# Parameters loaded with the first k-tiles, transposes placed behind ten products, other homes for three buffers, and a last output tile in two products of 256 columns

## The chip, the cores and the metric

The kernel runs on one NeuronCore of a Trainium2 chip. The metric is the device time of one execution in microseconds (us), lower is better. The engines are TensorE (PE in the profile; PEld is its weight load, which overlaps the products), VectorE (DVE), ScalarE (ACT), GpSimd (POOL) and SyncE (SP), on whose queue nearly all transfers are issued. Each engine and each queue works in the order in which its instructions stand.

## The reference

One layer of a streaming encoder on `x` of 1024 positions by 1024 features, all float32. One input projection gives four blocks of 512 columns: `u` for a diagonal state-space group (S5), `q` and `k` together, `v`, and a gate for a retention group of four heads. The parts around the change are these:

```python
lam_bar = jnp.exp(lam * dt); b_bar = ((lam_bar - 1.0) / lam)[..., None] * b
bu = jnp.einsum('blgc,gpc->blgp', u, b_bar)          # then an associative scan over positions
...
y = jnp.concatenate([y_s5, y_ret], -1) @ w_out
x = layer_norm(ALPHA * x + y, ln1_g, ln1_b)
ffn = (silu(conv3(x @ w_up_a)) * (x @ w_up_g)) @ w_down
x = layer_norm(ALPHA * x + ffn, ln2_g, ln2_b)
```

## The kernel before, in words

Every large product is made from float32 operands split into a high and a low part (ACT casts the high part, DVE subtracts it), three products of 128 rows by 512 columns for each pair of tiles (`mm3`, L132). The input projection runs block by block, `u` (block 0), `v` (2), `q,k` (1), gate (3), over four pairs of k-tiles (`project`, L195). For each pair `load_w` (L169) fetches two raw weight tiles through three rotating buffers `wraw` and splits them into `wsp<block>_<pair>`; in block 0 it fetches and splits `x` as well.

While `u` is multiplied, `load_constants` (L276, called by `project` after the second pair) puts the loads of the S5 parameters on SP, `par3` (lambda and step, 48 KB) first and `par` (B and C, 1 MB) later. DVE then works out powers of the discretised lambda in small operations of 32 to 256 columns (L324 to L407, scratch in `scr`), and from these the table `W` of two halves (L415 to L425): for each half a multiply into `W<h>`, a multiply into `Wt<h>`, and an add, 2048 columns each. The products of `u` leave PSUM in eight ACT copies into `U0` and `U1` (L293), go to a scratch `uscr` in DRAM in four stores (L294), two for each of `U0` and `U1`, and come back rearranged as `UT0`, `UT1` (L299). A load of `d` into the second quarter of `par` (L491, written far later in the program) has to wait until DVE has read that quarter in the two `Wt` multiplies (L422).

During the first two pairs of block `v` only seven of the eight PSUM banks hold `v`; through the eighth (`small`, L236) pass, between the products, eight `make_BT` (L447: four transposes of `W`, then one ACT copy into `BT0` or `BT1`; quarters 0 to 3 are BT0's) in the first pair and eight `make_V` (L461: products of `BT` with `UT`, ACT copies into `V2`) in the second. `spread_out(..., 5)` asks for one of them every five products, and the first pair has 42 products in all.

Buffers of 8 KB a partition come from an `Arena` (L73), a first-in first-out list of 20 slots: `free` puts a slot at the end, `get` takes the one that has been free longest, and the new tile's first writer waits for the last reader of the old one. Counted through, `BT0` takes the slot of `Wt1`, `BT1` that of `U0`, `wsp2_2` that of `U1`, `scan` that of `Wt0`.

The order of each engine's instructions is set when the program is built, by a planner: among the instructions that are ready on its own clock it takes the one that stands first in the program, with the weight loads and splits of blocks 1 to 3 moved ahead (`high_priority(HP)`). So an instruction written later can stand earlier in a queue when the planner believes it ready.

At the end (L1314 to L1327) four output tiles of 128 rows are completed one after the other, each by 33 products of 512 columns (`down_mm`) added to the high half of `zw[0][:, i]`. Ahead of them in the program stands `layer_norm_far` (L869) for four other tiles. Tiles 0 and 1 then use `layer_norm` (L863: DVE statistics, POOL's power -0.5, one DVE operation, one ACT scaling, one POOL addition), tiles 2 and 3 `layer_norm_last` (L886: the same statistics and power, then three DVE operations and two stores).

Of the kernel before, what the change touches and what calls it, by code (L numbers as in the profile page):

```python
# [12 lines left out]
F32 = mybir.dt.float32  # L13
F32R = mybir.dt.float32r
# [6 lines left out]
P = 128  # L21
# [7 lines left out]
EPS = 1e-5  # L29
# [77 lines left out]
def layer_kernel(ctx, tc, a, out):  # L107
# [87 lines left out]
    def project(blk, ops, banks, between=(), after=None, mid=None):  # L195


        ws = []
        late = len(between) > 0
        for kp in range(4):  # L200
            with tc.high_priority(0 if blk == 0 else HP):
                w, n = load_w(blk, kp)
            todo = deque(between[kp]) if late and kp < 2 else deque()
            ws.append(w)
            for q in range(2):
                k = 2 * kp + q
                if k < 7:
                    for (xi_, wi_) in ((0, 0), (0, 1), (1, 0)):
                        for j in range(7 if late and kp < 2 else 8):
                            l, r = ops(w[:, q], k, j, xi_, wi_)  # L210
                            T.matmul(banks[j], lhsT=l, rhs=r, start=(k == 0 and xi_ == 0 and wi_ == 0), stop=False)  # L211
                            if todo:
                                todo.popleft()()
                else:
                    for j in range(8):
                        proj3(banks[j], ops, w[:, q], k, j, False, True)
            assert not todo
            if mid is not None and kp == 1:
                mid()
            if late and kp < 2:  # L220
                if kp == 0:
                    continue
                if after is not None:
                    after()
                banks[7] = small("late")
                for k in range(4):
                    wk = ws[k // 2][:, k % 2]
                    proj3(banks[7], ops, wk, k, 7, k == 0, False)
                A.free(f"wsp{blk}_0")
            A.free(n)  # L230
            if blk == 3:
                A.free(f"x{2 * kp}", f"x{2 * kp + 1}")
# [11 lines left out]
    def spread_out(groups, n):  # L244

        return [g for gr in groups for g in [gr] + [lambda: None] * (n - 1)]
# [26 lines left out]
    pw = A.get([P, 2048], F32, "pw")  # L273
    par3 = pw[:, 1600:1696]

    def load_constants():  # L276
        SP.dma_start(par3, a["s5p"][:, 2048:S_END])
        SP.dma_start(con, a["con"])
        SP.dma_start(ident, a["ident"])
        SP.dma_start(par, a["s5p"][:, 0:2048])  # L280
        SP.dma_start(gains, a["gains"])
# [133 lines left out]

    A.free("scr")
    W = []
    for h in range(2):
        w_ = A.get([P, 16, 8, 16], F32, f"W{h}")
        t_ = A.get([P, 16, 8, 16], F32, f"Wt{h}")  # L420
        V.tensor_mul(w_, rev_pow(KR, 16 * h), vec_b(par[:, S_B1:S_B1 + 512], 16 * h))
        V.tensor_mul(t_, rev_pow(KIs, 16 * h), vec_b(par[:, S_B2:S_B2 + 512], 16 * h))  # L422
        V.tensor_add(w_, w_, t_)
        A.free(f"Wt{h}")
        W.append(w_)  # L425

    UT = []
    for h in range(2):
        UT.append(load_UT(h, f"UT{h}"))
        A.free(f"U{h}")  # L430

    scan = A.get([P, 4, 2, 256], F32, "scan")
    t1s = [scan[:, h] for h in range(2)]
# [27 lines left out]
    def make_V(i):  # L461
        h, q = i // 4, i % 4
        b_ = small(f"v{h}{q}")
        for e in range(4):
# [4 lines left out]


    banks = [bank(f"v_{b}") for b in range(7)] + [None]
    project(2, ops_b, banks, [spread_out([partial(make_BT, q) for q in range(8)], 5),
                              spread_out([partial(make_V, i) for i in range(8)], 5)])
    A.free("BT0", "BT1", "UT0", "UT1")
    vt = [A.get([P, 4, 512], F32, f"vt{h}") for h in range(2)]
# [120 lines left out]
    def glu_weights():  # L596
        r = A.get([P, 4, 512], F32, "glr")
        SP.dma_start(r, a["glu_w"])
        glh = A.get([P, 4, 512], F32R, "glh")
        gll = A.get([P, 4, 512], F32R, "gll")  # L600
        for k in range(4):
            S.copy(glh[:, k], r[:, k])
            V.tensor_sub(gll[:, k], r[:, k], f32(glh[:, k]))
        A.free("glr")
        return glh, gll

    glw = []
    banks = [bank(f"g_{b}") for b in range(8)]
    project(3, ops_b, banks, mid=lambda: glw.extend(glu_weights()))
    glh, gll = glw  # L610


# [250 lines left out]
    def layer_norm(z, lnv, pool, i):  # L863
        mv, rs = norm_stats(z, pool, i)
        V.scalar_tensor_tensor(z, z, mv[:, 0:1], lnv[:, 0], ALU.subtract, ALU.mult)
        S.activation(z, z, AF.Copy, scale=rs)  # L866
        G.tensor_add(z, z, lnv[:, 1])  # L867
# [446 lines left out]
    for m in range(NP):  # L1314
        down_prep_last(m)
    layer_norm_far([zw[1][:, i] for i in range(4)], lnv, cp, lambda i: SP.dma_start(outb(4 + i), zw[1][:, i]))
    for i in range(4):
        b_ = bank(f"dn3{i}")
        for m in range(NP):
            down_mm(b_, *dops[3, m], i, m == 0, m == NP - 1)  # L1320
        z, cs = zw[0][:, i], slice(512, 1024)
        V.tensor_add(z[:, cs], z[:, cs], b_)
        if i < 2:
            layer_norm(z, lnv, cp, f"b{i}")
            SP.dma_start(outb(i), z)
        else:
            layer_norm_last(z, lnv, cp, f"b{i}", lambda q, cs: (SP, S)[q].dma_start(outb(i)[:, cs], z[:, cs]))  # L1327


_ORDER = ["con", "ident", "xT", "xn", "w_in", "s5p", "d", "glu_w", "glu_b", "gains", "w_out",  # L1330
# [50 lines left out]
```

## Time and profile before

| | |
|---|---|
| median of 3 runs | 1027.43 us (1026.75 to 1028.75) |
| the profiled execution's own time | 1028.04 us |
| its span | 1026.3 us |
| PE busy in the span | 1004.3 us (98%) |
| DVE, ACT, POOL busy | 796.4, 447.7, 49.6 us |
| mean granted clock of TensorE | 0.993 of full speed |

All times in the rows are counted from the start of the span. A row of a timeline gives its start, the time from the first start to the last end of what was merged in it, the engine, the line, the operation, the tiles written and read, and, in brackets, how long the engine had been idle and which engine's instruction ended that.

### The profile page before, as it was taken

The page shows a single profiled execution, that of the slowest core. Times are in us where ns is not written, and L with a number is a line of the kernel's source. Part 1 is how long each engine was busy: PE and PEld are TensorE (multiplying, and loading weights), DVE is VectorE, ACT ScalarE, POOL GpSimd, SP SyncE. Part 2 cuts the span into 40 slices and gives each one's busy share as a digit, 9 for nine tenths or more (in the row PEclk, how much of TensorE's full clock was granted, in tenths as well). Part 3 has the DMA queues.
Part 4 walks back from the last instruction along what each step waited for, and adds up shares of the span by engine and source line. Part 5 has one row for each costly group of instructions (what it writes and reads, how often), then busy time and mean ns, then how long its engine had stood idle before and what let it go on. Part 6 is the DMA issues. An engine that isn't in the chain of part 4 may idle for free.

```text
span 1026.3 us, 12781 instructions
## 1 busy us (share of the span) xinstructions
PE 1004.3 (98%) x4748; PEld 828.7 (81%) x4748; DVE 796.4 (78%) x1376; ACT 447.7 (44%) x778; POOL 49.6 (5%) x60
## 2 busy tenths in 40 slices
PE   9989999999999999999999999999999999999996
PEld 7768887887777888788888888888888888888885
DVE  6937787727775599999878778778777896759987
ACT  4426302247562047554444444445444445444800
POOL 0000000002210150000000000000000000000003
PEclk9989999999999999999999999999999999999998
DMA  7362001261212223144232232322324996643113
GB/s 287 111 195 74 30 11 42 96 212 61 104 44 103 82 103 103 52 154 144 84 121 103 96 109 103 110 96 103 113 93 154 317 315 217 226 144 123 42 42 123
DMA packets 41934, 124.31 MB, mean 121 GB/s; under 512 B 4384, under 2 KB 10656, under 8 KB 37520
## 3 DMA queue, kind: packets, MB, share of 16 engines
q1 hardware_dynamic: 41584, 122.98, 34.4%
q8 instruction: 37, 0.61, 0.2%
q10 hardware_dynamic: 288, 0.52, 0.1%
q14 instruction: 25, 0.20, 0.1%
HBM read 92.32 MB, written 31.16 MB: 120 GB/s over the span
## 4 chain that ended last, share of the span: by engine, by line
PE 54%; DVE 5%; POOL 2%; issue 1%; DMA 1%; ACT 1%; POOLq 0%; DVEq 0%; SPq 0%
PE dn L134 6%; PE dn L135 6%; PE dn L133 6%; DVE ring L1007 1%; DVE XT L1234 1%; DMA wu<-in_w_up_dram 1%; POOL zw L867 1%; DMA wd<-in_w_down_dram 1%; POOL z L867 0%; DVE lbsf L877 0%; POOL lrsa L860 0%; DVE zw L1299 0%; POOL lrsb L860 0%; DVE zw L1306 0%; ACT z L866 0%
## 5 line engine op out<-in xcount | busy, mean ns | idle before, releaser
L1006 ACT CAST ring<-wu 128x512 fp32r<-128x512 f32 x130 | 80.0, 620 | 144.7 <-DMA wu<-in_w_up_dram 17.4
L1007 DVE TENSOR_TENSOR ring<-wu,ring 128x512 fp32r<-128x512 f32 x130 | 88.5, 687 | 21.4 <-ACT ring L1006 21.3
L134 PE MATMUL dn<-ring 128*128 128x512 f32 x264 | 102.9, 390 | 0.1
L135 PE MATMUL dn<-ring 128*128 128x512 f32 x264 | 102.8, 390 | 0.0
L133 PE MATMUL dn<-ring 128*128 128x512 f32 x264 | 102.8, 389 | 0.0
L1006 ACT CAST ring<-araw 128x512 fp32r<-128x512 f32 x66 | 41.1, 623 | 75.7 <-PE dn L134 61.8
L1007 DVE TENSOR_TENSOR ring<-araw,ring 128x512 fp32r<-128x512 f32 x66 | 45.3, 688 | 26.9 <-ACT ring L1006 26.9
L134 PEld LDWEIGHTS dn<-ring 128*128 128x128 f32 x264 | 49.6, 188 | 10.8 <-DVE ring L1007 0.5
L133 PEld LDWEIGHTS dn<-ring 128*128 128x128 f32 x264 | 49.6, 188 | 10.4
L135 PEld LDWEIGHTS dn<-ring 128*128 128x128 f32 x264 | 49.6, 188 | 10.1
L186 ACT CAST wsp<-wraw 128x512 fp32r<-128x512 f32 x32 | 19.1, 618 | 67.0 <-issue 49.7
L1007 DVE TENSOR_TENSOR ring<-wd,ring 128x512 fp32r<-128x512 f32 x66 | 44.9, 686 | 1.0 <-ACT ring L1006 1.0
L187 DVE TENSOR_TENSOR wsp<-wraw,wsp 128x512 fp32r<-128x512 f32 x32 | 21.4, 687 | 30.9 <-ACT wsp L186 30.8
L1006 ACT CAST ring<-wd 128x512 fp32r<-128x512 f32 x66 | 40.5, 617 | 7.8 <-DVE wd L1172 4.4
L211 PE MATMUL v<-wsp,x 128*128 128x512 f32 x147 | 41.3, 417 | 0.0
L211 PE MATMUL g<-wsp,x 128*128 128x512 f32 x168 | 40.1, 394 | 0.6 <-ACT qkT L589 0.6
L211 PE MATMUL u<-x,wsp 128*128 128x512 f32 x168 | 38.6, 391 | 0.6 <-ACT x L162 0.6
L211 PEld LDWEIGHTS u<-x,wsp 128*128 128x128 f32 x168 | 31.4, 188 | 8.0 <-ACT x L162 1.6
L211 PE MATMUL qk<-wsp,x 128*128 128x512 f32 x147 | 36.9, 395 | 0.0
L211 PEld LDWEIGHTS g<-wsp,x 128*128 128x128 f32 x168 | 30.8, 188 | 7.2 <-ACT qkT L589 1.3
L211 PEld LDWEIGHTS qk<-wsp,x 128*128 128x128 f32 x147 | 27.2, 188 | 6.4 <-ACT vt L477 0.9
L211 PEld LDWEIGHTS v<-wsp,x 128*128 128x128 f32 x147 | 27.8, 199 | 4.9
(1142 smaller groups left out, 2687.6 us busy)
## 6 DMA issues: line engine op xcount, KB each, us to landing
wu<-in_w_up_dram SPq DMA_DIRECT2D x22, 1024.0 KB, 4.9
araw<-hd SPq DMA_DIRECT2D x33, 512.0 KB, 3.8
wraw<-in_w_in_dram SPq DMA_DIRECT2D x32, 256.0 KB, 3.3
hd<-cg SPq DMA_DIRECT2D x22, 256.0 KB, 2.0
hd<-cg SPq DMA_DIRECT2D x11, 512.0 KB, 2.6
hd<-sS SPq DMA_DIRECT2D x11, 512.0 KB, 2.8
wd<-in_w_down_dram SPq DMA_DIRECT2D x11, 512.0 KB, 5.6
wd<-in_w_down_dram SPq DMA_DIRECT2D x22, 256.0 KB, 6.0
```

Of the source, the lines that this page charges most:

```text
L133: T.matmul(o, lhsT=lh, rhs=rh, start=first, stop=False)
L134: T.matmul(o, lhsT=lh, rhs=rl, start=False, stop=False)
L135: T.matmul(o, lhsT=ll, rhs=rh, start=False, stop=last)
L186: S.copy(t[:, q, 0], r)
L187: V.tensor_sub(t[:, q, 1], r, f32(t[:, q, 0]))
L211: T.matmul(banks[j], lhsT=l, rhs=r, start=(k == 0 and xi_ == 0 and wi_ == 0), stop=False)
L867: G.tensor_add(z, z, lnv[:, 1])
L1006: S.copy(t[:, 0], src)
L1007: V.tensor_sub(t[:, 1], src, f32(t[:, 0]))
L1234: V.tensor_sub(lo[:, ks], src[:, ks], f32(hi[:, ks]))
```

## The change

In the input stage: `load_constants` is called after the first pair of k-tiles as well, and then loads `par3` alone; all other parameters are loaded after the second pair as before. The two halves of `W` share one buffer `Wt`. `wsp2_2` gets its slot before `U0` and `U1` are freed. Counted through, `wsp2_2` now takes the slot of `scr`, `BT0` that of `U0`, `BT1` that of `U1`; `scan` takes that of `Wt`, and `UT0` and `UT1` take slots that earlier pairs of `x` and weights had used. In the first pair of `v`, ten products go ahead of the first `make_BT`, and the eight then follow at every fourth product (10 + 8 x 4 = 42).

At the end: tiles 0 to 2 all use `layer_norm_last`, with all stores on SP. Tile 3 is written out: statistics in four quarters of 256 columns, of which two are taken ahead of the products; two rounds of 33 products of 256 columns, each followed by its addition and statistics; the power on POOL; then four DVE operations of 256 columns, one of 512 and two of 256, with three stores.

```diff
-            if mid is not None and kp == 1:
-                mid()
+            if mid is not None and kp < 2:
+                mid(kp)
...
-    def load_constants():
-        SP.dma_start(par3, a["s5p"][:, 2048:S_END])
+    def load_constants(kp):
+        if kp == 0:
+            SP.dma_start(par3, a["s5p"][:, 2048:S_END])
+            return
         SP.dma_start(con, a["con"])
...
+    t_ = None
     for h in range(2):
         w_ = A.get([P, 16, 8, 16], F32, f"W{h}")
-        t_ = A.get([P, 16, 8, 16], F32, f"Wt{h}")
+        if h == 0:
+            t_ = A.get([P, 16, 8, 16], F32, "Wt")
         V.tensor_mul(w_, rev_pow(KR, 16 * h), vec_b(par[:, S_B1:S_B1 + 512], 16 * h))
         V.tensor_mul(t_, rev_pow(KIs, 16 * h), vec_b(par[:, S_B2:S_B2 + 512], 16 * h))
         V.tensor_add(w_, w_, t_)
-        A.free(f"Wt{h}")
         W.append(w_)
+    A.free("Wt")
...
     for h in range(2):
         UT.append(load_UT(h, f"UT{h}"))
-        A.free(f"U{h}")
+    ahead_w["wsp2_2"] = A.get([P, 2, 2, 512], F32R, "wsp2_2")
+    A.free("U0", "U1")
...
-    project(2, ops_b, banks, [spread_out([partial(make_BT, q) for q in range(8)], 5),
+    project(2, ops_b, banks, [[lambda: None] * 10 + spread_out([partial(make_BT, q) for q in range(8)], 4),
                               spread_out([partial(make_V, i) for i in range(8)], 5)])
...
-    project(3, ops_b, banks, mid=lambda: glw.extend(glu_weights()))
+    project(3, ops_b, banks, mid=lambda kp: glw.extend(glu_weights()) if kp == 1 else None)
...
-    for i in range(4):
+    for i in range(3):
         b_ = bank(f"dn3{i}")
         for m in range(NP):
             down_mm(b_, *dops[3, m], i, m == 0, m == NP - 1)
-        z, cs = zw[0][:, i], slice(512, 1024)
-        V.tensor_add(z[:, cs], z[:, cs], b_)
-        if i < 2:
-            layer_norm(z, lnv, cp, f"b{i}")
-            SP.dma_start(outb(i), z)
-        else:
-            layer_norm_last(z, lnv, cp, f"b{i}", lambda q, cs: (SP, S)[q].dma_start(outb(i)[:, cs], z[:, cs]))
+        z = zw[0][:, i]
+        V.tensor_add(z[:, HI], z[:, HI], b_)
+        layer_norm_last(z, lnv, cp, f"b{i}", lambda q, cs: SP.dma_start(outb(i)[:, cs], z[:, cs]))
+
+    z = zw[0][:, 3]
...
+    Q = [slice(256 * q, 256 * q + 256) for q in range(4)]
+    for q in range(2):
+        V.bn_stats(bs[:, q], z[:, Q[q]])
+    for q in (2, 3):
+        b_ = bank(f"dn33{q}")[:, 0:256]
+        for m in range(NP):
+            (lh, ll), (rh, rl) = dops[3, m]
+            ts_, cs = slice(3 * P, 4 * P), Q[q - 2]
+            mm3(b_, lh[:, ts_], ll[:, ts_], rh[:, cs], rl[:, cs], m == 0, m == NP - 1)
+        V.tensor_add(z[:, Q[q]], z[:, Q[q]], b_)
+        V.bn_stats(bs[:, q], z[:, Q[q]])
+    V.bn_aggr(mv, bs)
+    V.tensor_scalar(rs, mv[:, 1:2], EPS, None, ALU.add)
+    G.tensor_tensor(rs, rs, mh, ALU.pow)
+    for q in range(4):
+        V.scalar_tensor_tensor(z[:, Q[q]], z[:, Q[q]], mv[:, 0:1], lnv[:, 0, Q[q]], ALU.subtract, ALU.mult)
+    for q, cs in enumerate((LO, Q[2], Q[3])):
+        V.scalar_tensor_tensor(z[:, cs], z[:, cs], rs, lnv[:, 1, cs], ALU.mult, ALU.add)
+        (SP, S, SP)[q].dma_start(outb(3)[:, cs], z[:, cs])
```

## Rows read from the trace of the kernel before

**Rows 1.** The page, part 1: busy time and share of the span, by engine

```profile
PE 1004.3 (98%) x4748; PEld 828.7 (81%) x4748; DVE 796.4 (78%) x1376; ACT 447.7 (44%) x778; POOL 49.6 (5%) x60
```

**Rows 2.** Waits of PE over the whole span: in all, times, longest

```profile
PE bt L451 <- ACT BT L452: 3.1, 2, 2.6
```

**Rows 3.** Timeline of PE in block v

```profile
49.34 1.07 PE L211 MATMUL v<-wsp,x 128*128 128x512 f32 x4
52.85 0.63 PE L451 MATMUL bt<-ident,W 128*128 128x128 f32 x4 [2.44 <-issue]
...
57.63 0.60 PE L451 MATMUL bt<-ident,W 128*128 128x128 f32 x4
...
59.00 0.60 PE L451 MATMUL bt<-ident,W 128*128 128x128 f32 x4
...
63.35 0.88 PE L451 MATMUL bt<-ident,W 128*128 128x128 f32 x4 [2.59 <-ACT BT L452]
...
69.82 0.60 PE L451 MATMUL bt<-ident,W 128*128 128x128 f32 x4
```

**Rows 4.** PE by windows: stretch, busy us (instructions), granted clock, DMA share, GB/s

```profile
53.00:57.00 4.00, 3.45 (x14) 0.57 1.09 328
```

**Rows 5.** Timeline of ACT in the same stretch

```profile
44.78 5.35 ACT L293 COPY U<-u 128x512 f32<-128x512 f32 x8 [7.38 <-PE u L251]
55.06 0.59 ACT L452 COPY BT<-bt 128x512 f32<-128x512 f32 x1 [4.93 <-DVE pw L437]
...
61.68 1.14 ACT L186 CAST wsp<-wraw 128x512 fp32r<-128x512 f32 x2 [2.82 <-DMA uscr<-U]
```

**Rows 6.** Timeline of DVE: the table W

```profile
46.06 4.49 DVE L422 TENSOR_TENSOR Wt<-pw,par 128x2048 f32<-128x2048 f32 x2
50.47 4.49 DVE L423 TENSOR_TENSOR W<-W,Wt 128x2048 f32<-128x2048 f32 x2
```

**Rows 7.** Waits of SP's queue from 30 to 70 us

```profile
SPq L491 <- DVE Wt L422: 11.4, 1, 11.4
```

**Rows 8.** Timeline of SP's queue: start and length of issues

```profile
50.58 0.33 SPq L491 DMA_DIRECT2D par<-in_d_dram  x1
50.96 4.88 SPq L294 DMA_DIRECT2D uscr<-U  x4
57.12 0.36 SPq L299 DMA_DIRECT2D UT<-uscr  x1
```

**Rows 9.** DMA issues by line: count, KB each, median us from issue to landing

```profile
uscr<-U SPq DMA_DIRECT2D x4, 512.0 KB, 6.1
```

**Rows 10.** Timeline of PE: short products with their own weights, and the last product

```profile
71.88 1.05 PE L465 MATMUL v<-UT,BT 128*128 128x128 f32 x8
...
1016.52 0.39 PE L135 MATMUL dn<-last 128*128 128x512 f32 x1
```

**Rows 11.** Weight loads of the last tiles: count, busy us, mean ns, idle

```profile
L133 PEld LDWEIGHTS dn<-last 128*128 128x128 f32 x44 | 8.3, 188 | 1.7
```

**Rows 12.** Timeline of DVE at the end

```profile
1002.81 0.68 DVE L1322 TENSOR_TENSOR zw<-zw,dn 128x512 f32<-128x512 f32 x1
1003.40 1.28 DVE L857 BATCH_NORM_STATS2 lbsb<-zw 128x6 f32<-128x512 f32 x2
...
1016.83 1.41 DVE L891 SCALAR_TENSOR_TENSOR zw<-zw,lrsb,ln 128x512 f32<-128x512 f32 x2 [3.34 <-POOL lrsb L860]
1018.16 0.68 DVE L1322 TENSOR_TENSOR zw<-zw,dn 128x512 f32<-128x512 f32 x1
...
1019.99 1.28 DVE L888 SCALAR_TENSOR_TENSOR zw<-zw,lmvb,ln 128x1024 f32<-128x1024 f32 x1
1021.71 1.41 DVE L891 SCALAR_TENSOR_TENSOR zw<-zw,lrsb,ln 128x512 f32<-128x512 f32 x2 [0.44 <-POOL lrsb L860]
```

**Rows 13.** Timeline of POOL at the end

```profile
1013.90 2.39 POOL L867 TENSOR_TENSOR zw<-zw,ln 128x1024 f32<-128x1024 f32 x1 [1.26 <-ACT zw L866]
...
1020.22 1.46 POOL L860 TENSOR_TENSOR lrsb<-lrsb,mh 128x1 f32<-128x1 f32 x1 [3.42 <-DVE lrsb L859]
```

More of the change, by code (lines that the diff above doesn't have):

```diff
@@ L1320, in layer_kernel @@
             down_mm(b_, *dops[3, m], i, m == 0, m == NP - 1)
-        z, cs = zw[0][:, i], slice(512, 1024)
-        V.tensor_add(z[:, cs], z[:, cs], b_)
-        if i < 2:
-            layer_norm(z, lnv, cp, f"b{i}")
-            SP.dma_start(outb(i), z)
-        else:
-            layer_norm_last(z, lnv, cp, f"b{i}", lambda q, cs: (SP, S)[q].dma_start(outb(i)[:, cs], z[:, cs]))
+        z = zw[0][:, i]
+        V.tensor_add(z[:, HI], z[:, HI], b_)
+        layer_norm_last(z, lnv, cp, f"b{i}", lambda q, cs: SP.dma_start(outb(i)[:, cs], z[:, cs]))
+    z = zw[0][:, 3]
+    bs = cp.tile([P, 4, 6], F32, name="ebs")
+    mv = cp.tile([P, 2], F32, name="emv")
+    rs = cp.tile([P, 1], F32, name="ers")
+    Q = [slice(256 * q, 256 * q + 256) for q in range(4)]
[17 more added lines that the diff above has]
+        (SP, S, SP)[q].dma_start(outb(3)[:, cs], z[:, cs])
 _ORDER = ["con", "ident", "xT", "xn", "w_in", "s5p", "d", "glu_w", "glu_b", "gains", "w_out",
```

## The prediction

> **What bounds the kernel now.** The page's first part comes first: PE is busy 98% of the span [rows 1], so the time is PE's stream plus its few waits and what lies before and behind it. So the waits of PE come next. Those that the change touches stand at L451, the transposes of W: 3.1 us in two waits for ACT's copy of BT [rows 2], and 2.44 us at 52.85 [rows 3], together 5.5 us. The timeline of PE shows the stage: the first product of v starts at 49.34, the first transposes at 52.85, the fifth after 2.59 us of idleness at 63.35, the eighth at 69.82 [rows 3]. The windows then show a second loss: from 53 to 57 us the granted clock averaged 0.57 of full speed, so nearly all of it lay at the lower of the two levels, 1.2 instead of 2.4 GHz, right behind the first idle stretch [rows 4]; four such microseconds hold 1.7 us of lost work. Each wait is then followed to its cause. ACT's queue: the first copy of BT runs at 55.06, after DVE had finished with Wt1, whose slot BT0 has; two casts of wsp2_2 stand ahead of the fourth copy, for which the fifth transposes wait, and are held until 61.68 for the stores of U1, whose slot wsp2_2 has [rows 5]. The stores themselves are late because SP stood 11.4 us at the load of d [rows 7], which left at 50.58, when the two multiplies of L422 had read the old contents (46.06 + 4.49) [rows 6, 8]; only then went the four stores, although ACT's eight copies of u had run from 44.78 to 50.13 [rows 5, 8]. At the end, the timelines of DVE and POOL: the last product ends at 1016.9 [rows 10], its addition begins at 1018.16, because DVE stood 3.34 us for a power on POOL, which was behind the 2.39 us addition of L867 [rows 12, 13].
>
> **The change part by part.**
>
> *Stage v, if nothing waits.* A product takes 0.227 us (four in 1.07, the last one's 0.39 included [rows 3, 10]). Ten from 49.34 end at 51.6. W0 is ready by then: with one Wt the order becomes multiply, add, multiply, add, so the first add follows the first Wt multiply (46.06 + 2.2) and ends at 50.5 instead of 52.7 [rows 6]. One round of transposes, copy and four products is 1.37 us (57.63 to 59.00 [rows 3]). Seven rounds from 51.6 put the eighth transposes at 61.2 instead of 69.82: 8.6 us. In the two orders 38 and 36 products lie ahead of them: 0.45 us more. Together 9.05 us, which holds the 5.5 us of waits, the stretches at the lower clock and the two products; PE's stream behind it is the same, with hardly a wait in the profile to the tail, and its buffers follow PE, so I pass the gain on whole.
>
> *The homes.* The wait for Wt1 and the block of ACT's queue by wsp2_2 go. What is late next: ACT's copies into BT0 and BT1 now wait for the stores of U0 and U1. In the trace U0's had landed at 57.1 (UT0's load, which waits for them, leaves at 57.12) and U1's at 61.68 [rows 5, 8]. It hangs on where the planner puts the load of d. Before, it stands ahead of the stores; its release, the second L422 multiply, now comes one 2048-column operation of 2.2 us later [rows 6], up to 1.4 us more if wsp2_2's two splits go in between. That is about as much as the copies of one U half need (8 copies in 5.35 us [rows 5], so 2.7). If the stores pass it, U0's second leaves at about 47.5 and lands, 6.1 us from issue [rows 9], at 53.6, against 52.2 when the copy could start: a wait of 1.4 us, with less traffic none. U1's second leaves at 50.2, lands at 56.3, before BT1 is written (58); if the load of d slips in between, it lands at 59 to 60, up to 2.2 us late. I take 1.2 us from the range 0 to 2.2. Stage v: 9.05 - 1.2 = 7.8 us.
>
> *par3 one pair earlier.* DVE's chain to W may start some microseconds sooner, but DVE is nearly always busy from there on and cannot do the same work faster. PE doesn't wait for W at 51.6 any more, so I count 0; bounds: 0.3 us lost (the splits ahead of the first add) to nothing gained. The loads of the second pair move back by one issue, with several microseconds of products ahead of them.
>
> *The tail's products.* 66 of 256 columns replace 33 of 512, each with a weight load of its own. The trace has no such product. Nearest row: eight products with their own 128-column loads in 1.05 us, the last one's tail included [rows 10], at most 0.131 each; 0.115 without most of the tail. Then 66 take 7.6 us against 7.5 for 33, at most 8.6. The load's record is 0.188 us long [rows 11], so if one had to end within each product, 66 would take 12.4. I take 7.6: no difference.
> The Trainium skill (TensorE: Matmul & The Clock Gate, Part 3, "The mechanism") says that a weight load overlaps products in flight only where the row groups differ, and all of these use the same rows; load and product would then follow one another. The trace disagrees: a spacing of 0.227 us less a load of 0.188 would leave 0.039 us for 512 columns.
>
> *The tail's DVE.* Tiles 0 and 1 lose ACT's scaling and POOL's addition and get two DVE operations each. From 1002.81, when tile 0's addition starts, DVE now has until the last addition: three additions and six statistics at 0.6 (two in 1.28), three operations of 1024 columns at 1.2, six of 512 at 0.665 (1016.83 to 1018.16), 0.6 of small ones, and four of 256 columns at 0.35 (half of a 512's): 1.8 + 3.6 + 3.6 + 4.0 + 0.6 + 1.4 = 15.0, to 1017.8 without a wait [rows 12]. A power that POOL starts from rest takes 1.46 [rows 13], about 0.5 longer than the 1024-column operation beside it with the hand-over; three such waits unfilled make it 1019.3. I take 1018.3, against 1018.16: the queue on POOL goes, and DVE's own work stands in its place. PE's end at 1016.9 is hidden behind it, with 1.4 us to spare for slower short products.
> From that addition to the last scaling was 3.55 us (to 1021.71); an addition and a statistic of half the width save 0.3 each: 0.6. The last store is half as large: 0 to 0.5 us, I take 0.1. Tail: -0.1 + 0.6 + 0.1 = 0.6 us, from -0.5 to +1.4.
>
> *Sum.* 7.8 + 0.6 = 8.4 us. The profiled execution took 1028.04 (span 1026.3), so its counterpart is 1019.6. It is 0.6 above the median of the runs; against the median, 1019.0.
>
> **The rivals.**
>
> *A. The load of d still stands ahead of the stores.* For: it did, and its release moves by about as much as the stores have between them. Against: that release moves later, the copies of u do not. Then the stores leave D later than at 50.96; 2.2 from the order of W less what an earlier par3 gives, so D is about 0.5. The first copy ends at 57.7 + D, PE is idle from 52.9, and the clock falls behind it as after the first idle stretch (1.7 us): the second transposes come at 57.8 + D, the eighth six rounds (8.2) later, at 67.7 + D with the clock's part, a gain of 2.6 - D. With D 0.5 and the tail 2.7 us: 1024.7; D from -0.9 to 1.5 makes 1023.3 to 1025.7.
>
> *B. The same place, slower than before.* With wsp2_2's splits between the two halves of W and no earlier chain, D is 3.6, PE stands idle some 8 us and the clock stays at its lower level twice as long (another 1.7). Stage v loses 2.7, and with the tail the time is 1029.5. It decides from a D of 1.5 (clock low twice as long) to 3.2 (as in A). For: the copies now hang on stores that they didn't hang on; against: each part has to go the wrong way.
>
> *C. The short products pay for their loads.* At 0.188 each, 66 take 12.4 instead of 7.5; 1.4 of the 4.9 is hidden, so 1022.5. If load and half product (0.113) followed one another, 0.30 each, 19.9 us: 11 more than hidden, 1030.0, slower than before from 0.26 each on. For: loads as long as these never stood beside products as short; against: the eight in 1.05 us.
>
> *D. It doesn't do what it says:* the planner places the transposes otherwise, or the first copies wait though the stores left early; stage v gains 4 to 6, 1021 to 1023.
>
> **How the numbers follow.** Forecast 0.50, its own range 1017.0 (9.05 and the tail's 1.4) to 1021.5; A 0.27; B 0.06; C 0.06 at 1022.5 and 0.02 at 1030; D 0.09. From 1016.5 to 1025.5 lie nearly all of the forecast's 0.50 (0.47), 0.24 of A, 0.05 of C, 0.08 of D: 0.84, less the doubt in the parts, so some 8 in 10. 0.2% is 2 us, about what a measurement of this kernel tells from no change: faster is below 1025.4: 0.49 + 0.22 + 0.06 + 0.08 = 0.85, which I lower to 0.83; within 2 us: the rest of A and a third of B, 0.10; slower 0.07.
>
> **What would show it.** Right: in the timeline of PE the first transposes follow ten products at about 51.6 and the eighth come at 61 to 62.5; no window of block v with a clock below full; no wait of ACT's cast of wsp2_2; SP's stores begin at about 46. A: SP's queue still has L491's wait ahead of the stores, PE one idle stretch of about 5 us behind the first transposes, ended by ACT's copy. In the tail, starts of the short products 0.11 to 0.13 us apart, no L867 on POOL, and DVE without a gap of over 1 us before the last addition. The prediction is wrong if the products of block q,k start less than 5 us earlier than before, or if the tail, from the last product's end on, is over a microsecond longer.

## The result, and the profile after

The changed kernel takes 1018.29 us (median of 4 runs, 1016.78 to 1019.34), beside 1027.09 (1025.42 to 1028.75) for the kernel before on the same chip. The ratio is 0.9913, 95% interval 0.9891 to 0.9935: 8.9 us faster, 6.7 to 11.2. Predicted were 1019.0, with a range of 1016.5 to 1025.5. The profiled execution took 1019.34 (span 1017.6), so 8.70 less than the profiled one of before; predicted for it were 1019.6.

The busy time of PE is the first thing to read in the page of the changed kernel, against [rows 1]:

```profile
PE 1002.3 (99%) x4781; PEld 827.9 (81%) x4781; DVE 799.3 (79%) x1387; ACT 445.5 (44%) x776; POOL 45.2 (4%) x58
```

33 more products, 2 us less of busy time: in block v PE no longer spends time at the lower clock, as the windows below show. The timeline of PE in block v, against [rows 3]:

```profile
49.61 2.66 PE L211 MATMUL v<-wsp,x 128*128 128x512 f32 x11
52.11 0.60 PE L456 MATMUL bt<-ident,W 128*128 128x128 f32 x4
...
61.73 0.60 PE L456 MATMUL bt<-ident,W 128*128 128x128 f32 x4
...
63.10 1.06 PE L470 MATMUL v<-UT,BT 128*128 128x128 f32 x8
...
105.28 10.82 PE L211 MATMUL qk<-wsp,x 128*128 128x512 f32 x43
```

Eleven products, the first transposes, and then a round every 1.37 us without a wait; the eighth transposes at 61.73, where they stood at 69.82, and the first `make_V` (L470) at 63.10 instead of 71.88 [rows 10]. Block q,k begins at 105.28; in the kernel before it began at 113.74:

```profile
113.74 10.70 PE L211 MATMUL qk<-wsp,x 128*128 128x512 f32 x43
```

One window over the stage puts idle time and clock side by side (stretch; busy us and instructions of PE; granted clock; DMA share; GB/s), first before, then after:

```profile
50.00:75.00 25.00, 19.42 (x95) 0.86 0.63 200
```

```profile
50.00:75.00 25.00, 25.00 (x150) 1.00 0.52 170
```

The queues behind it. SP of the changed kernel, against [rows 8]:

```profile
46.51 4.79 SPq L296 DMA_DIRECT2D uscr<-U  x4
52.61 4.74 SPq L301 DMA_DIRECT2D UT<-uscr  x2
57.44 0.42 SPq L496 DMA_DIRECT2D par<-in_d_dram  x1
```

The four stores go first, and the load of d (now L496) stands behind them and behind the loads of `UT`: it holds back none of them. ACT, against [rows 5]:

```profile
42.74 1.14 ACT L186 CAST wsp<-wraw 128x512 fp32r<-128x512 f32 x2 [6.58 <-DVE pw L401]
45.05 5.35 ACT L295 COPY U<-u 128x512 f32<-128x512 f32 x8 [1.17 <-PE u L251]
52.79 0.59 ACT L457 COPY BT<-bt 128x512 f32<-128x512 f32 x1 [2.39 <-PE bt L456]
```

The casts of wsp2_2 stand ahead of the copies of u, and the first copy into BT0 waits for PE's transposes alone, not for the stores of U0.

At the end, DVE and then POOL of the changed kernel, against [rows 12, 13]:

```profile
995.57 0.68 DVE L1327 TENSOR_TENSOR zw<-zw,dn 128x512 f32<-128x512 f32 x1
...
1008.57 1.42 DVE L896 SCALAR_TENSOR_TENSOR zw<-zw,lrsb,ln 128x512 f32<-128x512 f32 x2
...
1010.24 0.41 DVE L1344 TENSOR_TENSOR zw<-zw,dn 128x256 f32<-128x256 f32 x1
...
1013.09 1.54 DVE L1352 SCALAR_TENSOR_TENSOR zw<-zw,ers,ln 128x512 f32<-128x512 f32 x3
```

```profile
1007.09 1.44 POOL L865 TENSOR_TENSOR lrsb<-lrsb,mh 128x1 f32<-128x1 f32 x1 [2.89 <-DVE lrsb L864]
1011.67 0.71 POOL L1348 TENSOR_TENSOR ers<-ers,mh 128x1 f32<-128x1 f32 x1 [3.14 <-DVE ers L1347]
```

DVE has no wait for POOL left. Three numbers carry the tail: from tile 0's addition to the last addition 14.67 us (before 15.35), from there to the last scaling 2.85 (3.55), from there to the end of the span 4.46 (4.54; the spans end at 1017.55 and 1026.25).

One new wait appears in PE's list of waits (in all, times, longest), at the first down product:

```profile
PE dn L134 <- DVE ring L1012: 0.8, 1, 0.8
```

The chain of waits puts it down to a load of `w_down` that took 6.21 us, 5.42 in the profile of before; of the twelve experiments below, par3_only and warm5 have it too, with 0.6 and 0.4, ten don't.

So the 8.70 us come from three stretches: 8.46 by the start of block q,k (8.73 in the stage itself, less 0.27 that v began later), 1.46 from tile 0's addition on, and 1.22 lost between them, 0.77 of it at that wait. Another 0.24 of the 1.22 belongs to the tail: the first product of the last four tiles starts at 979.35 (986.83 in the kernel before), and tile 0's addition comes 16.22 us behind it instead of 15.98. In the changed kernel a statistic of tile 3 stands ahead of that addition:

```profile
978.12 0.42 DVE L1337 BATCH_NORM_STATS2 ebs<-zw 128x6 f32<-128x256 f32 x1
```

All eight kernels with that block for tile 3 have the 16.22, the six others 15.98. Counted from the first product of the last four tiles, the tail takes 38.20 us instead of 39.42: it is worth 1.22, and 0.98 is lost ahead of it.

### The profile page after: what moved, and what is told of

It is laid out like the page before. It is cut to its first block, busy times and chain, and to the rows that moved or that the text cites. A ratio compares the mean times of both kernels' runs of the same rounds, so it can differ in the third digit from the quotient of the medians.

```text
span 1017.6 us, 12855 instructions
## 1 busy us (share of the span) xinstructions
PE 1002.3 (99%) x4781; PEld 827.9 (81%) x4781; DVE 799.3 (79%) x1387; ACT 445.5 (44%) x776; POOL 45.2 (4%) x58
## 4 chain that ended last, share of the span: by engine, by line
PE 84%; DVE 7%; ACT 3%; issue 2%; POOL 2%; DMA 2%; SPq 0%; DVEq 0%; POOLq 0%; ACTq 0%
PE dn L134 6%; PE dn L135 6%; PE dn L133 6%; PE g L211 4%; PE u L211 4%; PE qk L211 3%; PE v L211 3%; PE wb L133 1%; PE wb L134 1%; PE wb L135 1%; PE y L655 1%; PE y L656 1%; DVE XT L1239 1%; DVE ring L1012 1%; PE kern L492 1%
## 5 line engine op out<-in xcount | busy, mean ns | idle before, releaser
L1104 DVE SCALAR_TENSOR_TENSOR cg<-Ab,cv,cg 128x1024 f32<-128x1024 f32 x22 | 28.2, 1284 | 4.5 <-ACT cg L1103 4.5
```

What stands on the lines that cost most here:

```text
L1104: V.scalar_tensor_tensor(c, Ab[:, 1:1025], cv[:, f, 1:2], c, ALU.mult, ALU.add)
```

## The experiments

Every profile below was cut at the same four places: the first product of v, the first of q,k, the addition of tile 0, the end of the span. The lengths between them are worked out from the starts in the timelines of PE and DVE and from the end of the span to 0.01 us.

| kernel | time, us (runs) | before beside it | v to q,k | q,k to tile 0 | tile 0 to end |
|---|---|---|---|---|---|
| before | 1027.09 (4) | | 64.40 | 889.07 | 23.44 |
| after | 1018.29 (4) | 1027.09 | 55.67 | 890.29 | 21.98 |
| d_ahead | 1024.93 (10) | 1026.24 | 58.36 | 889.24 | 21.98 |
| d_pool | 1025.08 (1) | 1026.24 | 61.64 | 888.96 | 23.52 |
| par3_only | 1022.83 (1) | 1026.24 | 58.50 | 889.42 | 23.45 |
| ten_only | 1026.56 (1) | 1026.24 | 62.45 | 888.85 | 23.45 |
| front_only | 1019.73 (4) | 1026.59 | 55.67 | 888.76 | 23.46 |
| old_homes | 1020.81 (1) | 1026.59 | 56.15 | 889.11 | 21.99 |
| late_par3 | 1019.80 (1) | 1026.59 | 55.67 | 889.15 | 21.99 |
| no_ten | 1019.94 (1) | 1026.59 | 57.45 | 889.14 | 21.98 |
| tail_only | 1024.05 (7) | 1027.33 | 62.34 | 888.85 | 21.98 |
| tail_512 | 1018.70 (1) | 1027.33 | 55.63 | 888.94 | 22.63 |
| tail_pool | 1020.96 (1) | 1027.33 | 55.67 | 888.81 | 24.77 |
| warm5 | 1018.49 (5) | 1027.25 | 55.69 | 889.78 | 21.98 |

The middle column is the same work in all, and without the wait for `w_down` (after, par3_only, warm5) it lies within 0.5 us, the 0.24 of the new tail included. So the first and the last of the three columns can be read kernel by kernel, finer than the times.

**d_ahead: the changed kernel with the load of d forced ahead of the stores.**

```diff
-            SP.dma_start(<uscr, half h, part c>, t[:, c])        # in the loop that copies U
+        Us.append(t)
...                                                               # behind the table W
+    d_load = SP.dma_start(drep, a["d"].partition_broadcast(P))
+    with tc.issue_after(d_load.ins):
+        for h in range(2):
+            for c in range(2):
+                SP.dma_start(<uscr, half h, part c>, Us[h][:, c])
...                                                               # the load of d at its old place
-    SP.dma_start(drep, a["d"].partition_broadcast(P))
```

> The changed kernel with one thing forced: the load of d stands ahead of the four stores of U in SP's queue, as before the change. Theory (the order of that queue is the fork that decided the gain): the stores leave only when the second Wt multiply has ended, at about 53.6 us in the changed kernel's trace, so U0's land near 60 and U1's near 64.5; ACT's first copy into BT0 waits for U0's, PE stands idle from about 53.5 to 61 and then runs some microseconds at the lower clock. The first product of the late eighth column block, at 80.67 in the changed kernel and 89.13 before, then comes at 89.5 to 92, and the time is 1027 to 1029.5, no better than before. Rival (the gain comes from the ten products and the other homes by themselves, wherever the stores stand): that product stays within 3 us of 80.7 and the time below 1022.

Measured: 1024.93 (10 runs, 1023.00 to 1025.92), ratio to before 0.9986, 0.9977 to 0.9996: 1.4 us faster, where the whole change gives 8.9. Its tail is the changed one (21.98), so in the times the stretch up to block q,k has gained next to nothing. Both expectations missed: the first late product comes at 86.95, between the two, and so does the time. SP, ACT and PE of this kernel:

```profile
52.98 0.33 SPq L432 DMA_DIRECT2D par<-in_d_dram  x1
53.36 4.79 SPq L436 DMA_DIRECT2D uscr<-U  x4
```

```profile
59.53 0.59 ACT L465 COPY BT<-bt 128x512 f32<-128x512 f32 x1 [7.11 <-DMA uscr<-U]
```

```profile
54.12 0.60 PE L464 MATMUL bt<-ident,W 128*128 128x128 f32 x4
54.48 3.92 PE L211 MATMUL v<-wsp,x 128*128 128x512 f32 x16
60.17 0.66 PE L464 MATMUL bt<-ident,W 128*128 128x128 f32 x4 [1.77 <-ACT BT L465]
```

The stores leave at 53.36 instead of 46.51, and the first copy into BT0 is held until they land, at 59.53. PE stands only 1.77 us, because sixteen products, not four, were put ahead of the second transposes, and this execution shows a full clock behind it. That makes 2.7 us in the stage (58.36 to 55.67). So in this execution the stage is still 6.0 us shorter than in the profile of before; but block u took 46.15 us, 2.3 longer than there (see the last section). The profiled run is the shortest of the ten; where the median lost another 1.9 us no trace shows. The mean granted clock on record is 0.998 for the profiled run and 0.994 to 0.997 for the nine others, 0.994 for the two longest (1025.90 and 1025.92), which points to the lower clock for a part of it.

**d_pool: the kernel before with the load of d on POOL's queue.**

```diff
-    SP.dma_start(drep, a["d"].partition_broadcast(P))
+    G.dma_start(drep, a["d"].partition_broadcast(P))
```

> The kernel before with one thing changed: the load of d is issued from POOL's queue, which is idle there, so SP's four stores no longer stand behind it. Homes, order of the transposes and W are as before. Theory (the second idle stretch of 2.59 us came from the queue): the stores leave from 46 us, U1's land at about 57, the two casts of wsp2_2 find their slot free, PE's wait at the fifth transposes and the low clock behind it go; the wait for W at 52.85 stays. First late product at 84.5 to 86 instead of 89.13, time about 1023.5. Rival (the stores take until 61 whatever they wait for, because of the traffic of the stage): it stays at 88 to 89.5 and ACT's casts still wait beyond 60.

Measured: 1025.08 in one run. The stores leave at 45.90, and the stage is shorter than before by 2.8 us, not by more, as PE, ACT and the windows of PE show:

```profile
52.51 0.63 PE L451 MATMUL bt<-ident,W 128*128 128x128 f32 x4 [2.28 <-issue]
...
55.36 1.11 PE L451 MATMUL bt<-ident,W 128*128 128x128 f32 x4 [0.99 <-ACT BT L452]
```

```profile
54.72 0.59 ACT L452 COPY BT<-bt 128x512 f32<-128x512 f32 x1 [4.77 <-DVE pw L437]
```

```profile
53.00:57.00 4.00, 3.01 (x12) 0.57 0.93 207
57.00:61.00 4.00, 4.00 (x16) 0.58 0.98 385
```

With the stores early, the first copy still waits for DVE to be done with Wt1, whose slot BT0 has. PE stood 2.28 us for W before that, and the clock lay at the lower level for most of eight microseconds. The first late product came at 86.18, just behind the range of the theory. The rival fell: no cast of wsp2_2 waits for the stores.

**par3_only and ten_only: the kernel before with one edit each.** The first has the hunks of `mid(kp)` and `load_constants(kp)` of the change and nothing else; the second is this line alone:

```diff
-    project(2, ops_b, banks, [spread_out([partial(make_BT, q) for q in range(8)], 5),
+    project(2, ops_b, banks, [[lambda: None] * 10 + spread_out([partial(make_BT, q) for q in range(8)], 4),
```

> The kernel before with only the first part of the change: par3 loaded after the first pair. The prediction counted this part at 0. In the program's order for SP, though, this alone puts the four stores ahead of the load of d. Theory 1 (the part works through the queue): W is not more than 1 us earlier, PE still waits about 2 us at the first transposes, but the stores leave from 46 us and the second wait goes; first late product at 84.5 to 86, like the kernel with the load of d on POOL's queue; time about 1023.5. Theory 2 (the prediction's count): no change, 88.5 to 89.5.

> The kernel before with only the order of the transposes changed: ten products ahead of the first, then one at every fourth product. The load of d still stands ahead of the stores. Theory: the first wait, for W0, shrinks from 2.4 to about 1 us, but the first copy still waits for Wt1 (55.1) and the casts of wsp2_2, now behind the second copy, still wait until 61.7, so PE's idle time moves behind the third transposes and grows to 4 to 5 us; first late product at 88 to 90, no gain. Rival (the ten products alone hide the stage): 85 or less.

Measured: par3_only 1022.83, 3.4 us below the median beside it, by one edit that I had counted 0. SP's queue of that kernel shows why:

```profile
46.42 4.43 SPq L296 DMA_DIRECT2D uscr<-U  x4
...
61.09 0.42 SPq L493 DMA_DIRECT2D par<-in_d_dram  x1
```

With the parameters written one pair earlier the planner puts the load of d behind the stores. PE is left with two waits, 1.47 and 1.30 us, at full clock. The first late product comes at 83.57, earlier than theory 1 had it; theory 2, the prediction's count, fell. The stage is 3.1 us shorter than in d_pool, which has the same order of stores and load: there the first wait was 2.28 us and the clock fell behind it. Whether the earlier W or chance kept the clock up, one execution of each can't tell (in tail_only, with the late par3, the same wait was 1.26 us and the clock stayed full). ten_only gives nothing in its one run (1026.56), as its theory said: the d load stays ahead of the stores, and the wait only moves behind the third transposes, 3.88 us long, behind the casts that wait for the stores of U1. ACT's row:

```profile
60.39 1.14 ACT L186 CAST wsp<-wraw 128x512 fp32r<-128x512 f32 x2 [3.88 <-DMA uscr<-U]
```

**late_par3, old_homes and no_ten: the changed kernel with one edit taken back.**

```diff
# late_par3
-            if mid is not None and kp < 2:
+            if mid is not None and kp == 1:
...
-        if kp == 0:
-            SP.dma_start(par3, a["s5p"][:, 2048:S_END])
-            return
+        SP.dma_start(par3, a["s5p"][:, 2048:S_END])
# old_homes
-        if h == 0:
-            t_ = A.get([P, 16, 8, 16], F32, "Wt")
+        t_ = A.get([P, 16, 8, 16], F32, f"Wt{h}")
...
+        A.free(f"Wt{h}")
...
-    A.free("Wt")
...
-    ahead_w["wsp2_2"] = A.get([P, 2, 2, 512], F32R, "wsp2_2")
-    A.free("U0", "U1")
+        A.free(f"U{h}")
# no_ten
-    project(2, ops_b, banks, [[lambda: None] * 10 + spread_out([partial(make_BT, q) for q in range(8)], 4),
+    project(2, ops_b, banks, [spread_out([partial(make_BT, q) for q in range(8)], 5),
```

> The changed kernel with par3 loaded after the second pair, as before. In SP's order the stores stand ahead of the load of d all the same, since the second Wt multiply now comes behind the first add. Theory (par3 counts for nothing beside the shared Wt): W is ready some 0.9 us later, PE waits at most 1 us at the first transposes; first late product at 80.5 to 81.8. Rival (the chain to W needs the earlier start): 82.5 or later, with a wait of over 1.5 us at the first transposes.

> The changed kernel with the homes of before: a Wt buffer for each half, wsp2_2 in U1's slot, BT0 in Wt1's, BT1 in U0's. In SP's order the stores still stand ahead of the load of d. Theory (homes and order of W are worth 2 to 4 of the 8 us): the first copy waits for the second Wt read until about 54, the casts of wsp2_2 for U1's stores until about 57, each with copies behind it; first late product at 83 to 85 instead of 80.67. Rival (with the stores early the homes no longer matter): 80.5 to 81.5.

> The changed kernel with the transposes asked for at every fifth product from the start, as before. Theory: the first transposes come after 3 to 4 products and wait for W0 until about 51.3 (0.8 to 1 us), the first copy then waits a little for U0's stores, so PE loses 1 to 2 us in all: first late product at 81.7 to 82.8. Rival (the ten products are needed for the whole gain, because the idle stretch also brings the clock down): 84 or later, with a window below full clock.

Measured, from v to q,k: late_par3 55.67, nothing lost; old_homes 56.15, 0.5 lost; no_ten 57.45, 1.8 lost. In all three the stores leave ahead of the load of d. So the early par3 alone brings that order, and the new homes alone bring it too: each is enough, and with both one of them has nothing left to give. (old_homes and late_par3 have a longer block u in these executions, 46.49 and 45.73 us against 44.30, which is in their times and not in the column. By it alone the first late product of old_homes, at 83.31, lies in the range of the theory; from the start of v on its rival was nearer, 0.5 lost and not 2 to 4. The late product of late_par3, at 82.28, is late by the same cause; from v on its theory holds. So does that of no_ten.) In no_ten ACT shows what the ten products cover:

```profile
52.92 0.59 ACT L457 COPY BT<-bt 128x512 f32<-128x512 f32 x1 [2.52 <-DMA uscr<-U]
```

The first transposes come at 51.48 there, 0.81 us behind the last product, and are done by 52.1; the copy stands 0.8 us for the stores of U0. With ten products ahead it begins at 52.79, when they have landed.

**front_only and tail_only: the two halves of the change, each in the kernel before.**

> The changed kernel with the tail as before: only the edits of the input stage. Theory (the two halves of the change add up): first late product at about 80.7, last product of the kernel 8.2 us earlier than before, time 7.5 to 8.3 us below the kernel before. Rival (part of what stage v gives is lost behind it, and the tail gives the rest): less than 6 us.

> The kernel before with only the tail changed. Theory (the tail is worth what the two traces show, 1.66 us from the last product's end to the end of the span less 0.43 for the 66 short products): 0.8 to 1.6 us faster than before. Rival (the short products and DVE's extra work eat it): within 0.4 us of before.

Measured: front_only 1019.73, ratio 0.9939, 0.9922 to 0.9955: 6.3 us, 4.6 to 8.0. tail_only 1024.05, ratio 0.9979, 0.9964 to 0.9994: 2.2 us, 0.6 to 3.7; its profile says 1.46 (23.44 to 21.98), or 1.23 from the first product of the last four tiles (39.42 to 38.19). They add up to 8.5, beside 8.9 for the whole. front_only lies below its theory's 7.5 to 8.3 and above its rival's 6, with an interval that reaches into both. tail_only's 2.2 lies above its theory's range, its profile inside. tail_only also has the input stage of before, unchanged, and there its profile differs from that of before by 2.06 us (62.34 to 64.40). The window of PE in tail_only:

```profile
50.00:75.00 25.00, 19.96 (x108) 0.93 0.61 200
```

PE is idle nearly as long as in before (5.04 and 5.58 us), but the clock was low once (61 to 65 us) and not twice (53 to 57 and 63 to 67). So in this stage the profiled execution of before is two microseconds longer than another execution of the same instructions.

**tail_512 and tail_pool: the changed kernel with one half of the new tail.** In tail_512 all four tiles have 33 products of 512 columns and `layer_norm_last`; in tail_pool tile 3 is in halves, but tiles 0 and 1 keep ACT's scaling and POOL's addition.

```diff
# tail_512
-    for i in range(3):
+    for i in range(4):
...
# and the block of tile 3 left out
# tail_pool
-        layer_norm_last(z, lnv, cp, f"b{i}", lambda q, cs: SP.dma_start(outb(i)[:, cs], z[:, cs]))
+        if i < 2:
+            layer_norm(z, lnv, cp, f"b{i}")
+            SP.dma_start(outb(i), z)
+        else:
+            layer_norm_last(z, lnv, cp, f"b{i}", lambda q, cs: SP.dma_start(outb(i)[:, cs], z[:, cs]))
```

> The changed kernel with the last tile in 33 products of 512 columns and the norm that tiles 0 to 2 have, all stores on SP. Theory (halves shorten the chain behind the last product by more than the short products cost): PE ends 0.4 us earlier, but the addition and the statistic behind it are twice as wide and the last store is twice as large, so from the last product's end to the end of the span it is 8.3 to 9.0 us instead of 7.73, and the span is 0.3 to 0.9 longer against the start of the last 33 products. Rival (DVE was the bound, the halves only add to it): no longer, or shorter.

> The changed kernel with tiles 0 and 1 normed as before, with ACT's scaling and POOL's addition. Theory (the queue on POOL cost what DVE's own work now costs): POOL's power for tile 2 waits again behind an addition, DVE stands 1.5 to 3.3 us, the last addition begins 0 to 1 us later against the last product's end, so the span from there is 7.7 to 8.8 us instead of 7.73. Rival (taking DVE's extra 2.7 us away helps more than the queue costs): shorter than 7.6.

Measured, from the first product of the last four tiles to the end: before 39.42, tail_512 38.60, after 38.20 (38.19 to 38.22 in the seven kernels with this tail), tail_pool 40.99. So the move of tiles 0 and 1 to DVE, with all stores on SP, is worth 0.8 us by itself and the halved tile 0.4 on top of it; the halved tile without the move costs 1.6. (From tile 0's addition, as in the table, the halved tile looks 0.24 better.) From the last product's end to the end tail_512 takes 8.52 us, as its theory said; tail_pool takes 10.48, more than the 8.8 that its theory allowed. DVE and POOL of tail_pool:

```profile
1009.59 1.42 DVE L896 SCALAR_TENSOR_TENSOR zw<-zw,lrsb,ln 128x512 f32<-128x512 f32 x2 [4.60 <-POOL lrsb L865]
```

```profile
1000.47 3.45 POOL L872 TENSOR_TENSOR zw<-zw,ln 128x1024 f32<-128x1024 f32 x1 [1.26 <-ACT zw L871]
...
1006.66 2.39 POOL L872 TENSOR_TENSOR zw<-zw,ln 128x1024 f32<-128x1024 f32 x1 [1.26 <-ACT zw L871]
1009.01 0.55 POOL L865 TENSOR_TENSOR lrsb<-lrsb,mh 128x1 f32<-128x1 f32 x1
```

It is the wait of [rows 12], grown from 3.34 to 4.60 us: tile 2's power is behind the two additions on POOL, and every operation of the halved tile stands behind tile 2's scaling on DVE.

**warm5: the changed kernel with `range(5)` for `range(4)` at L266**, one more warm-up product ahead of u, because block u, the same products in every kernel, took 43.83 to 46.49 us.

> The changed kernel with five warm-up products instead of four ahead of the first product of u, so that TensorE has no gap between them. The question: in the profiles of this study the way from the first product of u to the first product of v lasted from 43.83 us (before) to 46.49, with the same products in it; in two of them (the one with the load of d forced ahead, 46.15, and the one with the late par3, 45.73) products stood about 0.45 us apart until 10 or 11 us though the granted clock was shown as full. Theory 1: the first products of u run at half pace because of the idle 0.4 to 0.7 us behind the warm-up; without it u starts some 0.5 us later (at 5.9), but the way from u to v is 43.8 to 44.0, the median falls by about half a microsecond, to 1017.5 to 1018.5, and the runs lie within 1.5 us of each other. Theory 2: it is the arrival of x and the weights that sets the pace of the first microseconds, whatever PE does before; then u starts 0.5 later, the way from u to v is as scattered as before (44.3 and more), the runs are spread over 2.5 us and the median is 1018.3 to 1019.

Measured: 1018.49 (1017.35 to 1018.90), ratio 0.9914, 0.9901 to 0.9928, the same as without it (0.9913). u starts at 5.47, not later than before, stands 0.25 us for x at 6.70, and takes 44.20 us. So neither theory is singled out: u doesn't start later, as both had it, and the median lies in both ranges. Its runs lie 1.55 us apart, those of the changed kernel 2.56, with so few runs too little to tell. No version that was run beats the changed kernel by more than its runs differ.

## Why the prediction was right

*The stage without a wait: 9.05 predicted, 8.73 measured.* Up to the first `make_V` the sum held: it comes 13.49 us behind the first product of v instead of 22.54, 9.05 less, with the round of 1.37 us as priced. (The first transposes follow eleven products and not ten, so the eighth gain 8.36 instead of 8.6; but 39 products and not 38 then lie ahead of them, and the two make up for each other.) The 0.3 that is missing is lost behind it, in the second pair. The first late product (of v's eighth column block) in the kernel before and in the changed one:

```profile
89.13 3.02 PE L251 MATMUL late<-wsp,x 128*128 128x512 f32 x12 [0.20 <-ACT V L468]
```

```profile
80.67 3.02 PE L251 MATMUL late<-wsp,x 128*128 128x512 f32 x12 [0.20 <-ACT V L473]
```

From the first `make_V` to there it is 17.57 us instead of 17.25. The new homes bring this: old_homes takes 17.29, the kernels with the homes of before 17.25 to 17.27, those with the new ones 17.55 to 17.59 (d_ahead, where products stand in another order, 17.11). Why they cost it stays open; ahead of the first `make_V` they win 0.8 (14.25 us from v in old_homes).

But 9.05 was taken from one execution. The same input stage in tail_only was 2.06 us shorter, and the times of front_only give 6.3. The terms that I priced at the lower clock were in that execution and are not in every one: of the 39 executions of the kernel before beside the experiments, the three with a mean granted clock of 0.993, that of the profiled one, took 1027.13 to 1028.11 us, the two with 0.998 took 1025.46 and 1026.06. So the stage is worth 6.3 to 6.9 by the times of front_only, and 8.5 only in this pair of profiles.

*The wait for U's stores: 1.2 predicted, none measured.* The stores left at 46.51 and landed sooner than in [rows 9], as the list of DMA issues of the changed kernel shows (KB each, median us to landing):

```profile
uscr<-U SPq DMA_DIRECT2D x4, 512.0 KB, 4.9
```

The mechanism was there: no_ten stands 0.8 us for them. The ten products hide it.

*par3 counted 0: right for the sum, wrong for the reason.* I looked for it in DVE's chain, and there it is worth 0.9 us at most (the first multiply of W at 40.04 instead of 40.94). What it moves is the place of the load of d in SP's queue. I left that place open as a question of the planner and gave the other answer rival A, without seeing which edit decides it; two do, each alone. Rival A's price held: 1024.7 predicted, 1024.93 for the kernel in which it is forced, but by luck: its execution in the trace has one wait of 1.8 us and a longer block u, the rest is unseen, and the long wait that I described isn't there.

*The short products: no difference predicted, 0.44 us measured, hidden.* The timeline of PE in the last tile of the changed kernel, and its weight loads (count, busy us, mean ns):

```profile
1001.79 0.28 PE L133 MATMUL dn<-last 128*128 128x256 f32 x1
1001.91 0.28 PE L134 MATMUL dn<-last 128*128 128x256 f32 x1
...
1009.59 0.28 PE L135 MATMUL dn<-last 128*128 128x256 f32 x1
```

```profile
L133 PEld LDWEIGHTS dn<-last 128*128 128x128 f32 x22 | 4.2, 192 | 0.0
```

65 spacings from 1001.79 to 1009.59 are 0.120 us each, 7.92 for 66, against 7.48 for 33 of 512. The loads, as recorded, are longer than a spacing, so they overlap the products of the same rows, and rival C falls. With it falls the sentence of the Trainium skill (TensorE: Matmul & The Clock Gate, Part 3, "The mechanism") that the prediction drew on, that loads overlap only where the row groups differ. The first paragraph of that section of the Trainium skill names a second case, a load into the background weight buffer. Whether this is one, no run here shows.

*The tail: 0.6 predicted, 1.46 measured from tile 0's addition, as it was summed, and 1.22 from the first product of the last tiles.* The first is 0.06 beyond the upper bound, the second, which is what the time gains, within it. The mis-sized term is DVE's stretch to the last addition: I put it at 15.5 us from tile 0's addition (to 1018.3), between 15.0 without a wait and 16.5 with three unfilled waits for POOL's power; it was 14.67, without a wait. One of the four 256-column operations that I counted in it, at 0.35, stood ahead of tile 0's addition, as shown above: 15.0 less 0.35 is 14.65. The waits didn't come: operations of other tiles (an addition, statistics) stand beside each power. So PE and DVE end together: the last product at 1009.87, the last addition 0.37 us later. The 0.6 from there on came out at 0.70, and the store at 0.08 for 0.1.

*What I had not: 0.98 us lost between block q,k and the last four tiles* (874.07 us instead of 873.09), most of it at the load of `w_down`. Nothing ties it to the change: ten of the twelve experiments have the same stream in 872.59 to 873.02, eight of them with the changed input stage or parts of it.

The sum of 8.4 was close because two errors cancel: in the pair of profiles, the stage gave 0.7 more than predicted (8.46 with v's later start) and the tail 0.6 more, and 1.0 went on the way. By the times of front_only the stage gave some 1 to 1.5 less than predicted, and by those of tail_only the tail 1.6 more, with an interval (0.6 to 3.7) that holds the 0.6 predicted and the 1.2 of the traces. So the main mechanisms were right, that of par3 was not, and that the sum came out so close was luck.

## What to carry to other kernels

When one transfer that waits stands ahead of others in a queue, find out what decides its place there, and test each edit for that alone: an edit that saves nothing on its own path can reorder another queue, and two edits that each do it don't add. Price the lower clock behind an idle stretch from more than one execution before you count it as a gain. Measure a stretch from an instruction that the change doesn't move: tile 0's addition was moved, and a cut there gave the tail 0.24 us too much. Where an engine at the end of the kernel is both a maker of a small value and a worker on large ones, look at the order of its queue: in tail_pool the shorter last step behind the same queue only waited longer.

## What the runs showed of the hardware

- The granted clock did not fall behind every idle stretch. It fell to the lower level behind those of 2.44 and 2.59 us in the kernel before, 2.28 in d_pool, 2.49 in tail_only and 3.88 in ten_only; it stayed full behind 1.47 and 1.30 in par3_only, 1.26 and 1.29 in tail_only, 1.21 in ten_only and 1.77 in d_ahead. But at the start of u in old_homes, with 0.69 us idle behind the warm-up and 0.94 three products later, it fell too (0.50 from 8 to 10 us), so the length of the last idle stretch alone doesn't tell.
- Block u can run slowly while the records show a full clock. In d_ahead the products stand 0.42 to 0.43 us apart until 10.75 us, where 0.23 is usual, and u takes 46.15 us; late_par3 is like it until 9.6. The same microsecond of d_ahead, and of the kernel before:

```profile
8.00:9.00 1.00, 1.00 (x3) 1.00 1.06 344
```

```profile
8.00:9.00 1.00, 1.00 (x7) 1.00 0.97 350
```

  In old_homes the products stand 0.42 to 0.43 us apart as well from 7.53 to 10.94 us, and there the records show the lower level. So the lower clock, unseen by the records, is a likely cause in d_ahead and late_par3 too; it is not shown. With one more warm-up product block u took 44.20 us, within the range without it.
- POOL's power took 0.71 us in the halved tile after 3.14 us of rest, 1.44 for tile 2 after 2.89. In tail_pool one took 1.53 straight behind an addition, the next 0.55. So rest alone, as I had read [rows 13], is not what makes the longer one. It stays open.
